# Issuing the rotary half copies from SyncE, and a planned order that runs the transposes of one PSUM tile in a row

## The chip, the cores and the metric

The kernel runs on one core of a Trainium2 chip. The core has five instruction queues that run side by side: TensorE (PE in the profile, with its weight loads shown apart as PEld), VectorE (DVE), ScalarE (ACT), GpSimd (POOL) and SyncE (SP), which here only issues DMAs. Each queue works through its instructions in the order in which they stand in the program; between queues, semaphores hold an instruction until its inputs are there. [...]

The metric is the device time of one execution in microseconds, as the median of three runs.

## What is computed

A two-layer backbone over 512 latent tokens and 256 context tokens of width 1024. Each layer normalises its input, projects it once into the queries, keys and values of three groups of heads and a gate, runs the three kinds of attention, multiplies by the gate and projects back:

```
def layer(x, cx, c_silu, cctx_silu, norm_w, ada_w, ada_b, w_in, w_out, qn, kn, rpb, sink, cos, sin, need_ctx):
    ...
    hx = rmsnorm(x, norm_w) * (1 + scale[:, None, :]) + shift[:, None, :]
    hc = rmsnorm(cx, norm_w) * (1 + scale_c) + shift_c
    px = split_cols(hx @ w_in)
    pc = split_cols(hc @ w_in)
    ya, yca = global_gqa(px[0], px[1], px[2], pc[0], pc[1], pc[2], cos, sin, qn, kn, need_ctx)
    yb, ycb = neighbourhood_attn(px[3], px[4], px[5], pc[3], pc[4], pc[5], rpb, need_ctx)
    yc_, ycc = window_gqa(px[6], px[7], px[8], pc[6], pc[7], pc[8], cos, sin, sink, need_ctx)
    ux = jnp.concatenate([ya, yb, yc_], axis=-1) * jax.nn.silu(px[9])
    x = x + gate[:, None, :] * (ux @ w_out)
```

Group A is global attention, group B attends to a two-dimensional neighbourhood, group C to a sliding window; all three also attend to the context. The queries and keys of A and C are rotated by position:

```
def apply_rope(x, cos, sin):
    x1, x2 = jnp.split(x, 2, axis=-1)
    ...
    return jnp.concatenate([x1 * c - x2 * s, x1 * s + x2 * c], axis=-1)
```

The first layer also updates the context; the second only reads it.

## The kernel before

**Numbers.** A float32 operand is kept as two parts (a rounded part and the rest), and a product takes three matmuls, rounded by rounded, rounded by rest and rest by rounded. The rounded part is made by ACT, the rest mostly by DVE or POOL.

**Stages.** The weights arrive in tiles of 256 KB (`ws`, line 251, and `ws` of the output projection, line 497), issued by SP into three buffers; ACT makes the rounded part `wh` (line 242), and DVE or POOL the rest `wl` (line 245), which frees the buffer. Projections run into two PSUM banks called `pj` (lines 308 and 329). The attention of one head runs in units: scores into `Sbig` (line 1028), a maximum on DVE (`negm`, lines 1133, 1183 and 1240), Exp on ACT into a tile `P` (lines 1135, 1186 and 1242), transposes of 128 x 128 blocks of `P` on PE into a PSUM tile `T` (line 1031, two banks), a copy out of `T` into a rounded part `pth` on ACT (line 778) and a rest `ptl` on DVE (line 1024), and the product with the values into `Obig` (line 1028). ACT's `otmp` (line 1046) and a sum on DVE take that product out. At the end of a pair of heads the gate and the sums of Exp are applied, again by way of transposes into `T` (lines 1326 and 1333 read them). Projections of later pairs are woven between these units, so that PE has work while it waits for an attention step.

**A tile of transposes.** In global attention a `T` tile takes four transposes, two from each of the two `P` tiles of a unit; in the other two groups two to four, from as many `P` tiles. These are float32 against `ident`. Queries and keys of group A are turned as well, in the rounded type against `identr` (lines 840 and 879), four to a tile. All four of a tile stand together in the program as written.

**Rotation of group C.** For a tile of queries or keys, ACT copies the projection out of PSUM into `tA` (line 953). A rotation needs the other half of each head, which lies in other partitions, so four DMAs of 32 partitions and 64 KB each copy `tA` into `tB` with the halves exchanged (line 958). POOL then multiplies `tA` and `tB` by the tables of cosines and sines and adds (lines 959 to 961); ACT and POOL make the two parts of the query from that (lines 969 and 970) or of the key (lines 979 to 981). There are ten such tiles: in each layer one of keys and four of queries. `tA` and `tB` have one buffer each, which the rotation of group A uses too.

**The order.** What each queue does first is not the order of the program text. After the whole program is recorded, `arrange` makes a `Step` of every instruction, with a cost (`Step.cost`: how long it holds its engine, `busy`, and when its result is there, `last`; for a DMA `busy` is the issue), builds the graph of what must come before what (`Graph.__init__`), and plays the program through (`Graph.run`): at each moment an engine takes the ready step of the best rank. Ranks come from playing the graph backwards from the end (`Graph.back`). This is done six times, and the order of the play with the earliest end is fixed as the order of every queue, the DMA issues of SP and ACT included.

Of the kernel before, what the change touches and what calls it, by code (L numbers as in the profile page):

```python
# [751 lines left out]
def mixers(tc, nc, l, last, p1, ps, const, env):  # L752
# [192 lines left out]
    def rope_c(s, scale, need_ctx, bank):  # L945
        q = p1.tile([128, NT], F32, name="tA", bufs=CFG["tA"])
        r = slot("tR")

        def done(p, c0, n):
            if c0:  # L950
                nc.scalar.activation(r[:, NT:NA], p, AF.Copy, scale=scale)
            else:
                nc.scalar.activation(rowmajor(q), colmajor(p), AF.Copy, scale=scale)  # L953

        yield from proj_f(l, s, need_ctx, bank, done)
        sw = p1.tile([128, NT], F32, name="tB", bufs=CFG["tA"])
        for b in range(4):
            nc.scalar.dma_start(sw[b * 32:(b + 1) * 32], q[(b ^ 1) * 32:((b ^ 1) + 1) * 32])  # L958
        en("cr0").tensor_mul(r[:, 0:NT], q, tabs["C", 0])
        en("cr1").tensor_mul(sw, sw, tabs["C", 1])  # L960
        en("cr2").tensor_add(r[:, 0:NT], r[:, 0:NT], sw)
        return r
# [511 lines left out]
    prev = None  # L1474
# [24 lines left out]
    for pair, items, n_ada in PLAN:  # L1499
# [3 lines left out]
        if pair is not None:  # L1503
            kind, i = pair
            if kind == "B":
                Q, K = made["b", i]
                prev = units("B", i, Q, K, made["v", i // 2][i % 2], lambda i=i: made["g", i // 2][i % 2], bmb)
            else:
                Q, G = made[kind.lower(), i]
                K, V = made[kind.lower() + "kv", 0]  # L1510
                prev = units(kind, i, Q, K, V, G, bmc if kind == "C" else None)
# [13 lines left out]
    prev = units("C", 3, Q, K, V, G, bmc)  # L1525
# [22 lines left out]
POOLS = ("p0_", "p1_0_", "p2_0_", "p1_1_", "p2_1_")  # L1548
BANKS = ("pj", "T", "Sbig", "Obig")
TO_PE, TO_OTHER, FIXED, RATE = 400.0, 150.0, 2550.0, 395.0  # L1550
WAIT = {"PE": 53.0, "POOL": 78.0, "ACT": 36.0, "DVE": 36.0, "SP": 30.0}
BEHIND = {"ACT": 112.0, "DVE": 85.0, "POOL": 45.0}


def stem(name):
    return name.rsplit("_", 1)[0]
# [9 lines left out]
class Step:  # L1566
# [16 lines left out]
    def cost(self):  # L1583
        ins = [u for u in self.use if not u[1]]
        outs = [u for u in self.use if u[1]]
        n = max([size(u[2]) for u in ins + outs[:1]] or [0])
        bank = any(stem(u[0].name) in BANKS for u in ins)
        op = str(getattr(self.inst, "op", getattr(self.inst, "func", ""))).split(".")[-1]
        e = self.engine
        self.plain = False  # L1590
        if self.dma:
            b = 4 * outs[0][2][0][1] * size(outs[0][2])
            self.busy = 330.0 if e == "SP" else 260.0
            self.move = 3460.0 if stem(outs[0][0].name) == "bc" else b / RATE
        elif e == "PE":
            n = size(ins[0][2])
            self.exact = ins[0][4] == "float32"
            self.busy = (108.0 if n == 128 else 230.0) if self.exact else max(n / 2.4 + 13.5, 66.0)
            self.last = 272.0 if self.exact else n / 2.4 + 180.0
        else:  # L1600
            if e == "ACT":
                d = 172.0 + 0.83 * n + (0 if bank else 35)
            elif e == "DVE":
                d = 156.0 + 0.52 * n if self.kind == "InstTensorCopy" and not bank else 152.0 + 1.06 * n
                self.plain = self.kind == "InstTensorTensor" and not bank and n >= 256
            elif op == "pow":
                d = 1000.0
            elif self.kind == "InstTensorScalarPtr":
                d = 440.0 + 2.2 * n if n > 8 else 190.0
            else:  # L1610
                d = 190.0 + 2.14 * n if n > 64 else 150.0
            self.busy = max(d - BEHIND[e], 20.0)
            self.last = d
            if e == "ACT" and op == "Exp" and n > 12:
                self.busy, self.last = d - 16, d + 91
# [18 lines left out]
class Graph:  # L1634


    def __init__(self, steps, tiles, needed):
        self.steps = steps
        n = len(steps)
        at = {s.name: k for k, s in enumerate(steps)}  # L1640
        self.before = [{} for _ in steps]
        seen, known, users, first = {}, {}, {}, {}
        for k, s in enumerate(steps):
            for tensor, writes, ap, offset, _ in s.use:
                name = tensor.name
                u = users.setdefault(name, [])
                if not u or u[-1] != k:
                    u.append(k)
                if name not in tiles or tiles[name][1]:
                    region, strict = None, writes  # L1650
                elif stem(name) in BANKS:
                    region, strict = (0, 128, 1), 1
                else:
                    if (ap, offset) not in known:
                        known[ap, offset] = cells(ap, offset)
                    region, strict = known[ap, offset], writes
                keep = []
                for rec in seen.get(name, ()):
                    r, st, w, j = rec
                    hit = region is None or (r[0] < region[1] and region[0] < r[1] and r[2] & region[2])  # L1660
                    if hit and (st or strict) and j != k:
                        t = steps[j]
                        full = 1
                        if t.engine == s.engine and not (t.dma or s.dma):
                            full = int(s.engine != "PE" and w)
                        elif region is None and w and writes:
                            full = 0
                        self.before[k][j] = max(full, self.before[k].get(j, 0))
                    over = (region is not None and hit and strict and region[0] <= r[0] and r[1] <= region[1]
                            and r[2] | region[2] == region[2])  # L1670
                    if not over or j == k:
                        keep.append(rec)
                keep.append((region, strict, writes, k))
                seen[name] = keep
        for a, b in needed:
            self.before[at[a]].setdefault(at[b], 0)
        self.users = {name: u for name, u in users.items() if name in tiles and not tiles[name][1]}
        for u in self.users.values():
            for k in u[1:]:
                self.before[k].setdefault(u[0], 0)  # L1680
        self.after = [[] for _ in steps]
        for k, b in enumerate(self.before):
            for j in b:
                self.after[j].append(k)
        self.tag = {name: tiles[name][0] for name in self.users}
        self.order = {}
        for name, u in sorted(self.users.items(), key=lambda x: x[1][0]):
            self.order.setdefault(self.tag[name], []).append(name)
        self.room = {t: min(CAPS.get(t.split("_")[0], 1), len(v)) for t, v in self.order.items()}
        self.place = {name: i for v in self.order.values() for i, name in enumerate(v)}  # L1690
        self.pool = {t: next((i for i, p in enumerate(POOLS) if "_" + p in t + "_"), None) for t in self.order}
        self.opens = [[] for _ in steps]
        for name, u in self.users.items():
            self.opens[u[0]].append(name)
        self.touch = [{u[0].name for u in s.use if u[0].name in self.users} for s in steps]

    def run(self, rank):

        steps, n = self.steps, len(self.steps)
# [4 lines left out]
        now = {e: [] for e in ENGINES.values()}  # L1704
# [8 lines left out]
            if self.pool[t] is not None:  # L1713
                stage_left[self.pool[t]] += len(v)
        lanes, pipe = [], 0.0
        done = 0

        def push(k):
            heapq.heappush(later[steps[k].engine], (ready[k], rank[k], k))
# [9 lines left out]
        while done < n:  # L1729
            t, e = min((max(free[e], -1.0 if now[e] else later[e][0][0]), e) for e in later if now[e] or later[e])  # L1730
            free[e] = t = max(t, free[e])
            while later[e] and later[e][0][0] <= t:
                _, r, k = heapq.heappop(later[e])
                heapq.heappush(now[e], (r, k))
            r, k = heapq.heappop(now[e])
            s = steps[k]
            need, wait = t, None
# [24 lines left out]
            busy = s.busy  # L1762
            if s.dma:
                pipe = fin = max(t + FIXED, pipe) + s.move
                lanes.append(fin)
            elif e == "PE":
                fin = t + s.last
            else:
                extra = 0.55 * min(free["POOL"] - t, s.last) if s.plain and free["POOL"] > t else 0.0
                fin = t + s.last + extra  # L1770
                busy += extra
# [18 lines left out]
            for j in self.after[k]:  # L1790
                x = fin + self.gap(s, steps[j]) if self.before[j][k] else t
# [173 lines left out]
```

## Time and profile before

| | |
|---|---|
| median of three runs | 1178.56 us (1177.38 to 1178.78) |
| profiled execution | 1178.53 us |
| its span, first to last instruction | 1176.3 us |
| mean granted TensorE clock | 0.996 |
| matmuls | 8016 |
| transposes in float32 of `P` (line 1031) | 1024 |
| transposes of group A's queries and keys (lines 840, 879) | 48 and 80 |
| copies of rotary halves | 40, on ACT's queue |

In rows of busy time an engine's figure is the time in which at least one of its instructions runs, with the count behind an x. Matmuls overlap: one of 256 columns is drawn 0.28 us long and the next may start 0.12 us after it. In a timeline row stand the start, the length, the engine (with a q where its sequencer issues or waits and the engine itself does nothing), the line, the operation, the tiles as out<-in, the shapes and the count; in square brackets is the idle time of that engine just before, and what ended it. In a row of waits stand who waited, for whom, the sum in us, how often, and the longest.

### The profile page before, as it was taken

What the parts mean: (1) busy time and instruction counts of PE and PEld (TensorE: products, weight loads), DVE (VectorE), ACT (ScalarE), POOL (GpSimd) and SP (SyncE); (2) the same over time, 40 slices, a digit from 0 to 9 for tenths busy, and PEclk for the clock granted to TensorE, in tenths of its full rate; (3) what the DMA queues carried; (4) which work ended last, traced back from release to release, by engine and by line L of the source; (5) the groups of instructions that cost most, each with busy time, mean ns of one, the idle gap of its engine ahead of it and who ended that gap; (6) DMA issues with size and microseconds to landing.
All of it is one profiled execution on the core that took longest, in us unless ns stands there. A gap on an engine that the chain in (4) does not pass through costs nothing. (4 is left out here: it accounts for less than half of the span.)

```text
span 1176.3 us, 21720 instructions
## 1 busy us (share of the span) xinstructions
PE 1141.1 (97%) x8016; PEld 1028.0 (87%) x8016; DVE 766.3 (65%) x1548; ACT 697.8 (59%) x1581; POOL 401.7 (34%) x496
## 2 busy tenths in 40 slices
PE   5999999999999999999999999999999999999996
PEld 3799989998898898988788999989988989898885
DVE  5667666665455665657979855676665566668652
ACT  5447555566557666678723634555656677778641
POOL 2442111125445456367300030221235665466001
PEclk9999999999999999999999999999999999999998
DMA  9633222213222222122577432233221121123152
GB/s 359 209 99 99 83 70 95 101 55 112 81 69 96 72 77 86 59 64 91 157 253 265 153 129 88 88 98 98 88 79 60 58 72 53 57 63 108 37 170 72
DMA packets 60825, 124.21 MB, mean 106 GB/s; under 512 B 7216, under 2 KB 13488, under 8 KB 60720
## 3 DMA queue, kind: packets, MB, share of 16 engines
q1 hardware_dynamic: 54768, 111.96, 29.8%
q10 hardware_dynamic: 5952, 10.88, 2.8%
q8 instruction: 63, 1.03, 0.4%
q14 instruction: 42, 0.34, 0.1%
HBM read 109.05 MB, written 11.14 MB: 102 GB/s over the span
## 5 line engine op out<-in xcount | busy, mean ns | idle before, releaser
L1024 DVE TENSOR_TENSOR ptl<-T,pth 128x512 fp32r<-128x512 f32 (+2 forms) x312 | 181.4, 591 | 119.3 <-ACT pth L778 114.7
L778 ACT ACTIVATE pth<-T 128x512 fp32r<-128x512 f32 (+2 forms) x312 | 160.7, 522 | 103.5 <-PE T L1031 93.1
L329 PE MATMUL pj<-wh,hL 128*128 128x256 f32 x896 | 189.2, 289 | 0.2 <-DVE vt L854 0.2
L308 PE MATMUL pj<-hL,wh 128*128 128x512 f32 x544 | 186.4, 405 | 0.0
L1031 PE MATMUL T<-ident,P 128*128 128x128 f32 x1024 | 177.9, 274 | 5.7 <-DVE ptl L1024 2.8
L1028 PE MATMUL Sbig<-kt,qt 128*128 128x256 f32 (+1 forms) x864 | 162.0, 309 | 1.2 <-DVE negm L1240 0.8
L242 ACT ACTIVATE wh<-ws 128x512 fp32r<-128x512 f32 x192 | 120.2, 630 | 67.3 <-PE pj L308 16.2
L1031 PEld LDWEIGHTS T<-ident,P 128*128 128x128 f32 x1024 | 124.8, 140 | 29.3 <-DVE ptl L1024 8.1
L329 PEld LDWEIGHTS pj<-wh,hL 128*128 128x128 f32 x896 | 147.3, 190 | 2.1 <-issue 1.3
L245 POOL TENSOR_TENSOR wl<-ws,wh 128x512 fp32r<-128x512 f32 x76 | 98.4, 1300 | 122.4 <-ACT wh L242 115.6
L1028 PE MATMUL Obig<-ptl,vt 128*128 128x256 f32 (+2 forms) x432 | 131.1, 317 | 1.4 <-DVE ptl L1024 1.4
L1028 PEld LDWEIGHTS Sbig<-kt,qt 128*128 128x128 f32 x864 | 124.8, 189 | 7.8 <-DVE negm L1240 1.4
L1028 PE MATMUL Obig<-pth,vt 128*128 128x256 f32 (+2 forms) x432 | 130.0, 309 | 1.4 <-ACT pth L778 1.2
L329 PE MATMUL pj<-wl,hL 128*128 128x256 f32 x448 | 128.3, 287 | 0.0
L245 DVE TENSOR_TENSOR wl<-ws,wh 128x512 fp32r<-128x512 f32 x116 | 82.5, 721 | 41.7 <-ACT wh L242 31.9
L308 PEld LDWEIGHTS pj<-hL,wh 128*128 128x128 f32 x544 | 97.1, 189 | 13.9 <-ACT wh L242 0.4
L308 PE MATMUL pj<-hL,wl 128*128 128x512 f32 x272 | 109.0, 401 | 0.1
L1028 PEld LDWEIGHTS Obig<-pth,vt 128*128 128x128 f32 x432 | 81.8, 189 | 7.8 <-ACT pth L778 2.0
L1028 PEld LDWEIGHTS Obig<-ptl,vt 128*128 128x128 f32 x432 | 81.6, 189 | 6.6 <-DVE ptl L1024 2.2
L329 PEld LDWEIGHTS pj<-wl,hL 128*128 128x128 f32 x448 | 85.2, 190 | 1.0 <-issue 0.4
L1413 POOL TENSOR_TENSOR bm<-wr,bm 128x192 f32<-128x192 f32 (+1 forms) x48 | 36.6, 789 | 136.5 <-DMA bm<-mskB_dram 73.2
L1047 DVE TENSOR_TENSOR OT<-Obig,otmp 64x512 f32<-64x512 f32 (+1 forms) x88 | 45.1, 512 | 49.2 <-ACT otmp L1046 48.3
(336 smaller groups left out, 2522.5 us busy)
## 6 DMA issues: line engine op xcount, KB each, us to landing
ws<-wf_dram SPq DMA_DIRECT2D x72, 256.0 KB, 2.9
ws<-wt_dram SPq DMA_DIRECT2D x72, 256.0 KB, 2.9
ada<-adaw_dram SPq DMA_DIRECT2D x32, 512.0 KB, 5.5
ws<-wo_dram SPq DMA_DIRECT2D x57, 256.0 KB, 2.9
bm<-mskB_dram SPq DMA_DIRECT2D x16, 576.0 KB, 3.5
dots<-adat_dram SPq DMA_DIRECT2D x16, 256.0 KB, 3.1
dw<-adat_dram SPq DMA_DIRECT2D x8, 512.0 KB, 7.3
u<-u ACTq DMA_DIRECT2D x9, 384.0 KB, 2.5
```

What stands on the lines that cost most here:

```text
L242: nc.scalar.activation(hi, src, AF.Copy)
L245: eng.tensor_sub(lo, src, hi.bitcast(F32))
L308: nc.tensor.matmul(p[:, 0:n], a[:, r, :], cols(b[kt], c0, n), start=(i == 0), stop=(i == 23))
L329: nc.tensor.matmul(p[:, t * 256:(t + 1) * 256], tok(a[kt], t2 + t), b[:, r, :], start=(i == 0), stop=(i == 23))
L778: nc.scalar.activation(out, src, AF.Copy)
L1024: nc.vector.tensor_sub(lo[:, 0:n], T[:, 0:n], hi[:, 0:n].bitcast(F32))
L1028: return nc.tensor.matmul(*args, **kw)
L1031: return nc.tensor.transpose(*args, **kw)
L1047: nc.vector.tensor_add(OT[64 * h:64 * h + 64, c0:c0 + n], O[0:64, 0:n], tmp[:, 0:n])
L1413: nc.gpsimd.tensor_add(b, src, b)
```

## The change

Line 958 issues the four copies from `nc.sync` in place of `nc.scalar`. All else is in the planner:

- The cost of a DMA issue was 330 ns on SP and 260 ns on ACT. It is now looked up by the name of the tile written: 580 for `tB`, 680 for `wr`, 430 for all other tiles here (no tile of this kernel is named `R5` or `R2`).
- A matmul of 128 columns in the rounded type holds PE for 65.3 ns in the plan, where it was 66.8. Where a matmul follows a transpose, 5 ns (float32) or 86 ns (rounded type) are added.
- Transposes that stand together in the program and write the same PSUM tile form a run. Each of them now has to wait for all that any of them needs, and while one of a run has just been taken, the plan takes the next ready one of the same run before anything else.

```diff
--- before.py
+++ after.py
@@ -955,7 +955,7 @@
         yield from proj_f(l, s, need_ctx, bank, done)
         sw = p1.tile([128, NT], F32, name="tB", bufs=CFG["tA"])
         for b in range(4):
-            nc.scalar.dma_start(sw[b * 32:(b + 1) * 32], q[(b ^ 1) * 32:((b ^ 1) + 1) * 32])
+            nc.sync.dma_start(sw[b * 32:(b + 1) * 32], q[(b ^ 1) * 32:((b ^ 1) + 1) * 32])
         en("cr0").tensor_mul(r[:, 0:NT], q, tabs["C", 0])
         en("cr1").tensor_mul(sw, sw, tabs["C", 1])
         en("cr2").tensor_add(r[:, 0:NT], r[:, 0:NT], sw)
@@ -1548,6 +1548,7 @@
 POOLS = ("p0_", "p1_0_", "p2_0_", "p1_1_", "p2_1_")
 BANKS = ("pj", "T", "Sbig", "Obig")
 TO_PE, TO_OTHER, FIXED, RATE = 400.0, 150.0, 2550.0, 395.0
+ISSUE = dict(tB=580.0, R5=520.0, R2=520.0, wr=680.0)
 WAIT = {"PE": 53.0, "POOL": 78.0, "ACT": 36.0, "DVE": 36.0, "SP": 30.0}
 BEHIND = {"ACT": 112.0, "DVE": 85.0, "POOL": 45.0}
 
@@ -1587,16 +1588,18 @@
         bank = any(stem(u[0].name) in BANKS for u in ins)
         op = str(getattr(self.inst, "op", getattr(self.inst, "func", ""))).split(".")[-1]
         e = self.engine
-        self.plain = False
+        self.plain, self.turn, self.switch = False, None, 0.0
         if self.dma:
             b = 4 * outs[0][2][0][1] * size(outs[0][2])
-            self.busy = 330.0 if e == "SP" else 260.0
+            self.busy = ISSUE.get(stem(outs[0][0].name).split("_")[0], 430.0)
             self.move = 3460.0 if stem(outs[0][0].name) == "bc" else b / RATE
         elif e == "PE":
             n = size(ins[0][2])
-            self.exact = ins[0][4] == "float32"
-            self.busy = (108.0 if n == 128 else 230.0) if self.exact else max(n / 2.4 + 13.5, 66.0)
-            self.last = 272.0 if self.exact else n / 2.4 + 180.0
+            exact = ins[0][4] == "float32"
+            self.turn = outs[0][0].name if stem(ins[0][0].name) in ("ident", "identr") and n == 128 else None
+            self.switch = 5.0 if exact else 86.0
+            self.busy = (108.0 if n == 128 else 230.0) if exact else n / 2.4 + (13.5 if n > 128 else 12.0)
+            self.last = 272.0 if exact else n / 2.4 + 180.0
         else:
             if e == "ACT":
                 d = 172.0 + 0.83 * n + (0 if bank else 35)
@@ -1674,6 +1677,20 @@
                 seen[name] = keep
         for a, b in needed:
             self.before[at[a]].setdefault(at[b], 0)
+        run = []
+        for k in [k for k, s in enumerate(steps) if s.engine == "PE"] + [None]:
+            if run and (k is None or steps[k].turn is None or steps[k].turn != steps[run[0]].turn):
+                whole = {}
+                for i in run:
+                    for j, full in self.before[i].items():
+                        if j < run[0]:
+                            whole[j] = max(full, whole.get(j, 0))
+                for i in run:
+                    for j, full in whole.items():
+                        self.before[i][j] = max(full, self.before[i].get(j, 0))
+                run = []
+            if k is not None and steps[k].turn:
+                run.append(k)
         self.users = {name: u for name, u in users.items() if name in tiles and not tiles[name][1]}
         for u in self.users.values():
             for k in u[1:]:
@@ -1713,7 +1730,7 @@
             if self.pool[t] is not None:
                 stage_left[self.pool[t]] += len(v)
         lanes, pipe = [], 0.0
-        done = 0
+        prev, done = None, 0
 
         def push(k):
             heapq.heappush(later[steps[k].engine], (ready[k], rank[k], k))
@@ -1732,6 +1749,12 @@
             while later[e] and later[e][0][0] <= t:
                 _, r, k = heapq.heappop(later[e])
                 heapq.heappush(now[e], (r, k))
+            if e == "PE" and prev is not None and prev.turn:
+                same = [x for x in now[e] if steps[x[1]].turn == prev.turn]
+                if same:
+                    now[e].remove(min(same))
+                    heapq.heapify(now[e])
+                    heapq.heappush(now[e], ((-1e18, 0), min(same)[1]))
             r, k = heapq.heappop(now[e])
             s = steps[k]
             need, wait = t, None
@@ -1765,6 +1788,10 @@
                 lanes.append(fin)
             elif e == "PE":
                 fin = t + s.last
+                if not s.turn and prev is not None and prev.turn:
+                    busy += prev.switch
+                    fin += prev.switch
+                prev = s
             else:
                 extra = 0.55 * min(free["POOL"] - t, s.last) if s.plain and free["POOL"] > t else 0.0
                 fin = t + s.last + extra
```

## The prediction

> **What bounds the kernel now.** I read the page's first two parts, then the busy time by stretch, the list of DMA issues, the line of the half copies, and the timeline around each of their bursts.
>
> ```profile
> PE 1141.1 (97%) x8016; PEld 1028.0 (87%) x8016; DVE 766.3 (65%) x1548; ACT 697.8 (59%) x1581; POOL 401.7 (34%) x496
> ```
>
> ```profile
> 0.00:30.00 30.00, 17.10 (x108) 9.90 (x108) 17.80 (x52) 16.27 (x36) 7.19 (x12) 1.00 0.97 359
> 30.00:1160.00 1130.00, 1118.46 (x7869) 1013.24 (x7868) 744.22 (x1487) 680.38 (x1543) 389.68 (x478) 1.00 0.31 99
> 1160.00:1176.30 16.30, 5.58 (x43) 4.86 (x41) 4.26 (x9) 1.19 (x3) 4.84 (x7) 0.68 0.38 129
> ```
>
> PE is busy for 97% of the span, at a granted clock of 1.00 (the third number from the right) until the last stretch. The change leaves every matmul in place, so it can win only where PE waits. The rows by stretch say where: 30.00 - 17.10 = 12.90 us at the start, where the DMA engines are 97% busy; 16.30 - 5.58 = 10.72 us in the closing chain; and 1130.00 - 1118.46 = 11.54 us in the whole middle. Start and end have no rotary copy and hardly a transpose. So what this change can win lies in those 11.54 us, plus a little that the rows hide: a 256-column matmul is drawn 0.28 us long while the next one starts 0.12 us after it, so every idle figure is about 0.16 us short of what PE loses.
>
> **Part one: the half copies leave ACT.**
>
> ```profile
> L958 ACTq DMA_DIRECT2D tB<-tA x40: 514/593/858, 275.8 to 1065.2; - x40
> ...
> DMA to landing us min/median/max: 1.9/2.0/3.8
> ```
>
> Ten rotary tiles with four copies each are 40 issues with a median of 593 ns; a tile's four hold ACT for about 2.4 us, 24 us in all. ACT has room for that over the span (59% busy), but it does its work in a fixed order, and what stands behind a burst is late by the burst. This is the worst one:
>
> ```profile
> 878.39 2.46 ACTq L958 DMA_DIRECT2D tB<-tA  x4
> ...
> 879.90 0.28 PE L308 MATMUL pj<-hC,wh 128*128 128x256 f32 x1
> 880.90 0.38 ACT L778 ACTIVATE pth<-T 128x256 fp32r<-128x256 f32 x1 [2.54 <-DMA tB<-tA]
> ...
> 881.33 0.39 PE L1028 MATMUL Obig<-pth,vt 128*128 128x256 f32 x1 [1.16 <-ACT pth L778]
> ```
>
> ACT issues from 878.39 to 880.85; only then can it copy a transposed tile out of PSUM (pth), and PE, which needs pth, has nothing from 879.90 + 0.12 until 881.33: 1.31 us lost, where the row shows 1.16 idle. Four other bursts end in a wait of PE:
>
> ```profile
> 278.38 0.38 ACT L1046 ACTIVATE otmp<-Obig 64x256 f32<-64x256 f32 x1 [1.85 <-DMA tB<-tA]
> ...
> 279.81 0.63 PE L1031 MATMUL T<-ident,P 128*128 128x128 f32 x4 [0.88 <-DVE u L1333]
> ```
>
> ```profile
> 376.53 0.38 ACT L1046 ACTIVATE otmp<-Obig 64x256 f32<-64x256 f32 x1 [2.54 <-DMA tB<-tA]
> ...
> 377.96 0.63 PE L1031 MATMUL T<-ident,P 128*128 128x128 f32 x4 [0.94 <-DVE OT L1326]
> ```
>
> ```profile
> 526.57 0.60 ACT L778 ACTIVATE pth<-T 128x512 fp32r<-128x512 f32 x1 [1.25 <-issue]
> ...
> 527.95 0.66 PE L1031 MATMUL T<-ident,P 128*128 128x128 f32 x4 [0.64 <-DVE ptl L1024]
> ```
>
> ```profile
> 955.50 0.50 PE L1028 MATMUL Sbig<-kt,qt 128*128 128x256 f32 x2 [0.42 <-ACT P L1135]
> ```
>
> In the first two ACT's otmp stands behind the burst, DVE's sum behind otmp, and a PSUM bank that DVE must read first behind that; in the third ptl stands behind a pth that ACT took up between two issues; in the fourth the Exp of line 1135 came late. Idle: 1.16 + 0.88 + 0.94 + 0.64 + 0.42 = 4.04 us, and with 5 x 0.16 us hidden, 4.8 us. The other five bursts show no wait of PE that carries a sum; I round to **5 us**. All of it should go, since in these rows nothing but the issues keeps ACT. What is late next at those places I cannot see; if it is late by half as much, 2.5 us remain of the gain. Those are the ends for this part: 2.5 and 5.5.
>
> **What SP pays.** SP issues its own loads at 0.33 us each and otherwise waits:
>
> ```profile
> 872.62 0.33 SPq L251 DMA_DIRECT2D ws<-wf_dram  x1
> 883.20 17.65 SPq L251 DMA_DIRECT2D ws<-wt_dram  x4
> ```
>
> ```profile
> SPq L251 <- POOL wl L245: 298.5, 52, 21.9
> ```
>
> Around the worst burst SP has nothing to issue from 872.95 to 883.20. No row shows such a copy on SP; I take ACT's 0.59 us, so 24 us on a queue that spent 298.5 us on one kind of wait alone. Behind a copy that waits for its tile (line 953, on ACT) stand the weight loads, and for them ACT's split; a burst delays them by 2.4 us, and those loads are queued several tiles ahead. I cost it at nothing; without that cover it would be 2.4 us for a tile. The other way round, a copy may stand behind a load that waits up to 21.9 us for its buffer. Who waits for a late copy is POOL's rotation, then the query tile, then PE's band scores:
>
> ```profile
> 909.45 2.45 ACTq L958 DMA_DIRECT2D tB<-tA  x4
> ...
> 918.66 1.29 POOL L970 TENSOR_TENSOR qt<-tR,qt 64x512 fp32r<-64x512 f32 x1
> ...
> 920.42 0.28 PE L1028 MATMUL Sbig<-kt,qt 128*128 128x256 f32 x1
> ```
>
> ```profile
> 1082.26 1.29 POOL L970 TENSOR_TENSOR qt<-tR,qt 64x512 fp32r<-64x512 f32 x1 [0.52 <-ACT qt L969]
> ...
> 1091.36 0.88 DVE L1183 CUSTOM_DVE_ANT_0 P<-Sbig,msk,negsink 128x640 f32<-128x640 f32 x1
> ```
>
> The first query tile of layer 1 is ready at 919.95, and PE reads it 0.47 us later; the last one is ready at 1083.55, and the first reduction of its scores starts 7.8 us later. So the copies have cover everywhere but at 909, and there the price of landing at the slow end (3.8 against 2.0 us) is 1.8 - 0.47 = 1.3 us at most, if PE finds nothing else; it has projection matmuls, so I take 0.
>
> A rule speaks against the move. The Trainium skill, "DMA: Bandwidth & Descriptors", section "Issuing engines are not separate DMA queues", says that DMAs share the same 16 DMA engines whoever issues them, and that spreading them saves only issue time; its section on queues, rings and completion order adds that an engine alternates between queue rows and starts one row's descriptors in order. The landing row (2.0 median, 3.8 at most) fits the sharing. By the rule a copy on SP's row starts behind a weight load instead of beside it, and the sum would lose up to that same 1.3 us at 909 and nothing elsewhere.
>
> **Part two: the order.** The planner's costs change for every DMA issue, and the transposes of one PSUM tile now run in a row, none before all their inputs are there. First what a broken row costs PE:
>
> ```profile
> 916.56 0.60 PE L1031 MATMUL T<-ident,P 128*128 128x128 f32 x4
> ...
> 917.48 0.27 PE L1031 MATMUL T<-ident,P 128*128 128x128 f32 x1
> 917.50 0.36 PE L329 MATMUL pj<-wh,hL 128*128 128x256 f32 x1
> 917.71 0.28 PE L329 MATMUL pj<-wl,hL 128*128 128x256 f32 x1
> ```
>
> ```profile
> 236.11 0.22 PE L840 MATMUL T<-identr,qd 128*128 128x128 f32 x1
> 236.17 0.34 PE L329 MATMUL pj<-wl,hC 128*128 128x256 f32 x1
> 236.34 0.28 PE L329 MATMUL pj<-wh,hC 128*128 128x256 f32 x1
> ...
> 236.81 0.37 PE L840 MATMUL T<-identr,qd 128*128 128x128 f32 x3
> ```
>
> Within a row a float32 transpose takes (0.60 - 0.27)/3 = 0.11 us. A single one between matmuls takes 917.71 - 917.48 - 0.12 = 0.11 us as well: breaking a row costs nothing. With identr it is (0.37 - 0.22)/2 = 0.075 us in a row and 236.34 - 236.11 - 0.12 = 0.11 us alone, 0.035 us for a break; there are 128 of them in 32 tiles, and if every one stood alone the 96 breaks would be worth 3.4 us. Most stand in threes and fours in the stretches I read; I take **0.5 us**, between 0 and 3.4.
>
> Against that stands a wait. A global-attention tile takes its transposes from two probability tiles, and the second is ready one Exp later:
>
> ```profile
> L1135 ACT ACTIVATE P<-Sbig,negm 128x768 f32<-128x768 f32 x64 | 57.7, 901 | 22.4 <-DVE negm L1133 20.5 <-ACT wh L242 0.8 <-DVE ptl L1024 0.6
> L1135 ACT ACTIVATION_READ_ACCUMULATOR P<-Sbig,negm 128x1 f32 x64 | 12.6, 197 | 0.0
> ```
>
> That is 0.90 + 0.20 = 1.10 us in each of 64/2 = 32 pairs: 35 us if PE had nothing else, 0 if projection matmuls fill it. Now they fill nearly everything (11.54 us idle in 1130), and the planner places its rows with that filler, so I take 0 and keep a quarter of the pairs, 8 x 1.1 = 8.8 us, as the far end that I would still believe. Behind a waiting transpose all of PE's later work stands; next it is pth and ptl.
>
> Last, the new costs re-sort all queues. What an order leaves outside the five waits is 11.54 - 4.04 = 7.5 us; a new order draws this anew, between 0 and twice that. I take no change.
>
> Sum against the profiled execution's own 1178.53 us (span 1176.3 and 2.2 around it; the median of the runs, 1178.56, is the same): 1178.53 - 5.0 - 0.5 = 1173.0 us.
>
> **The rivals.**
> - **The new order also fills other waits.** Most of the 7.5 us goes, because the planner's picture of the queues is truer: 1173.0 - 5 = 1168.0 us. For it: the waits at the bursts look like errors of its picture. Against it: what is left is small waits on DVE, which the change does not cost anew.
> - **The order gives the gain back.** ACT, freed, meets DVE or a PSUM bank a little later, and about as much new idle time appears elsewhere: 1173.0 + 4.5 = 1177.5 us. For it: with two T banks and one Obig the chain has little play. Against it: PE ran through the other five bursts with hardly a wait.
> - **The rows hold PE (slower).** Place: the first transposes of a pair's tile in global attention, where PE has to wait for the second Exp. Price 1.10 us for each pair without filler; the 5.5 us are gone from the fifth, and the time is over 1180.9 from the eighth: 1173.0 + 8.8 = 1181.8 us. Against it: the filler is there in both layers.
> - **A copy is late on SP's queue** at 909, by the queue or by a load in front: 1173.0 + 1.3 = 1174.3 us; a load that holds it by 10 us would cost more, but the planner orders SP by the same times.
>
> **How the numbers follow.** Forecast 0.45 (1170.5 to 1175.8), fills other waits 0.17 (around 1168), late copy 0.06 (1174.3), gain given back 0.18 (1177.5), rows hold PE 0.14 (1181.8). About 0.2%, 2.4 us, is what a measurement can tell from no change, so faster is below 1176.2 and slower above 1180.9. Faster: 0.45 + 0.17 + 0.06 = 0.68, to which the given-back case adds 0.02 from its low end: 0.70. Same: the rest of that case, 0.16. Slower: 0.14. The range runs from 1166.5 (the second case less 1.5) to 1181.8 (eight pairs held), leaving about 0.07 below and 0.11 above.
>
> **What would show it.** In the profile after: the line of the copies on SPq, 40 of them; no ACT row whose idle time ends with a copy's issue; PE's idle time in the middle at about 6 to 7 us; the transposes of a tile in one row of four or three. Wrong would be: PE waits on P of line 1135 in front of rows of transposes (the slower case), as much idle time in the middle as before with other releasers (given back), POOL's line 960 waiting long for the copies with PE idle at the first band scores (late copy), or a start or end stretch that moves, which I costed at nothing.

## The result, and the profile after

The median of five runs is 1174.18 us (1172.83 to 1175.16) against 1178.56 us before: a ratio of 0.9962, with a 95% interval from 0.9950 to 0.9974. The forecast was 1173.0 us. The time was foreseen, but the profile after does not look as the forecast said. The page's busy time, and the busy time by stretch (columns as before):

```profile
PE 1138.2 (97%) x8016; PEld 1031.2 (88%) x8016; DVE 764.4 (65%) x1548; ACT 699.5 (60%) x1581; POOL 405.6 (35%) x496
```

```profile
0.00:30.00 30.00, 16.31 (x114) 9.36 (x116) 18.05 (x53) 17.03 (x37) 9.03 (x12) 1.00 0.96 351
30.00:1156.00 1126.00, 1115.53 (x7861) 1016.29 (x7856) 742.02 (x1487) 681.20 (x1542) 391.74 (x478) 1.00 0.31 99
1156.00:1172.40 16.40, 6.32 (x48) 5.59 (x47) 4.33 (x9) 1.30 (x4) 4.86 (x7) 0.75 0.37 128
```

The span fell by 3.9 us, from 1176.3 to 1172.4. In the middle stretch PE is idle for 1126.00 - 1115.53 = 10.47 us, where it was 11.54 and where I had expected 6 to 7. Start and end changed by 0.8 us up and 0.6 us down. The other 3.0 us are in PE's busy time, which also holds waits too short to show beside the drawn length of a matmul. At the five bursts of the forecast PE no longer waits, but other waits came. The largest of the new ones, in the timeline of after:

```profile
277.10 2.49 SPq L958 DMA_DIRECT2D tB<-tA  x4
...
279.69 0.72 SPq L195 DMA_DIRECT2D ada<-adaw_dram  x1
...
280.67 0.33 SPq L251 DMA_DIRECT2D ws<-wt_dram  x1
...
283.63 1.27 POOL L960 TENSOR_TENSOR tB<-tB,tabx 128x512 f32<-128x512 f32 x1 [2.99 <-DMA tB<-tA]
...
288.68 1.71 ACT L979 ACTIVATE kt<-tR 64x768 fp32r<-64x768 f32 x2 [3.08 <-POOL tR L961]
...
289.61 4.49 POOL L980 TENSOR_TENSOR kt<-tR,kt 64x768 fp32r<-64x768 f32 x2 [0.96 <-ACT kt L979]
...
291.47 0.95 DVE L981 CAST kt<-kt 64x1536 fp32r<-64x1536 f32 x1 [5.15 <-POOL kt L980]
292.46 0.42 DVE L1047 TENSOR_TENSOR OT<-Obig,otmp 64x256 f32<-64x256 f32 x1
...
292.93 0.38 PE L1028 MATMUL Obig<-pth,vt 128*128 128x256 f32 x1 [1.61 <-DVE OT L1047]
...
293.76 0.55 PE L308 MATMUL pj<-hC,wh 128*128 128x256 f32 x1 [0.45 <-DVE mod L221]
```

This is layer 0's tile of rotary keys. Its copies are issued on SP by 279.59, but POOL gets the last of them only at 283.6, 4 us later, with a 512 KB load and a weight load in flight beside it. From there the delay walks down the chain: POOL's rotation, ACT's rounded key, POOL's rest, and DVE's copy of line 981. DVE works in order and stood idle for 5.15 us in front of that copy, with the sum of line 1047 behind it; PE could not write `Obig` until that sum had read it, and its next projection waited 0.45 us more for DVE's line 221. Then the clock fell (columns: the stretch and its length, PE's busy time and count, granted clock, DMA share, GB/s):

```profile
290.00:292.00 2.00, 1.32 (x11) 1.00 0.00 0
292.00:294.00 2.00, 0.62 (x2) 0.92 0.00 0
294.00:296.00 2.00, 2.00 (x10) 0.50 0.00 0
296.00:298.00 2.00, 2.00 (x15) 0.73 0.00 0
298.00:300.00 2.00, 2.00 (x19) 1.00 0.03 8
```

From 294 to 296 PE is drawn busy all the time and gets 10 matmuls done, against 19 in the 2 us from 298, at full clock. A stretch like this counts as busy, so PE's idle time alone hides it.

### The profile page after: what moved, and what is told of

Its sections match the earlier page's. It is cut to its first block, busy times and chain, and to the rows that moved or that the text cites. A ratio compares the mean times of both kernels' runs of the same rounds, so it can differ in the third digit from the quotient of the medians.

```text
span 1172.4 us, 21741 instructions
## 1 busy us (share of the span) xinstructions
PE 1138.2 (97%) x8016; PEld 1031.2 (88%) x8016; DVE 764.4 (65%) x1548; ACT 699.5 (60%) x1581; POOL 405.6 (35%) x496
## 5 line engine op out<-in xcount | busy, mean ns | idle before, releaser
L329 PE MATMUL pj<-wh,hL 128*128 128x256 f32 x896 | 186.0, 286 | 0.0
L308 PE MATMUL pj<-hL,wh 128*128 128x512 f32 x544 | 181.4, 401 | 0.0
L1031 PE MATMUL T<-ident,P 128*128 128x128 f32 x1024 | 162.4, 274 | 5.4 <-DVE ptl L1024 4.3
L1031 PEld LDWEIGHTS T<-ident,P 128*128 128x128 f32 x1024 | 121.4, 140 | 26.2 <-DVE ptl L1024 8.4
L1133 DVE TENSOR_REDUCE negm<-Sbig 128x1 f32<-128x768 f32 x64 | 61.1, 955 | 28.2 <-ACT P L1135 14.8
```

The source lines that it names most:

```text
L308: nc.tensor.matmul(p[:, 0:n], a[:, r, :], cols(b[kt], c0, n), start=(i == 0), stop=(i == 23))
L329: nc.tensor.matmul(p[:, t * 256:(t + 1) * 256], tok(a[kt], t2 + t), b[:, r, :], start=(i == 0), stop=(i == 23))
L1031: return nc.tensor.transpose(*args, **kw)
L1133: nc.vector.tensor_reduce(nm, S, axis=AX.X, op=OP.max, negate=True)
```

## The experiments

The theory was that of the forecast: ACT's issues held PE. Its rivals were the rows of transposes, the late copy, and the costs by which the order is made. All times are medians against runs of the kernel before on the same chip, whose medians were 1178.98, 1179.07 and 1179.64 us in the three groups; ratios are used to compare across groups.

| run | time us | ratio to before | 95% interval |
|---|---|---|---|
| e1 order of before, 40 copies on SP | 1178.87 | 0.9994 | 0.9983 to 1.0004 |
| e2 order of after, 40 copies on ACT | 1173.01 | 0.9950 | 0.9937 to 0.9962 |
| e4 after without the rule for rows | 1171.44 | 0.9938 | 0.9925 to 0.9950 |
| e5 rule for rows alone | 1184.39 | 1.0048 | 1.0034 to 1.0061 |
| e7 order of after, layer 0's key tile on ACT | 1171.37 | 0.9937 | 0.9924 to 0.9949 |
| e8 order of before, 36 copies on SP | 1173.16 | 0.9953 | 0.9941 to 0.9966 |
| e9 issue costs alone | 1168.32 | 0.9913 | 0.9899 to 0.9926 |
| e10 costs of PE alone | 1180.66 | 1.0015 | 1.0007 to 1.0024 |
| e11 issue costs and the move | 1173.33 | 0.9943 | 0.9930 to 0.9955 |
| e12 cost of a copy alone | 1170.07 | 0.9919 | 0.9906 to 0.9933 |
| e13 issue costs with 330 for the rest | 1171.35 | 0.9926 | 0.9913 to 0.9938 |
| e14 order of e9, 36 copies on SP | 1169.10 | 0.9909 | 0.9896 to 0.9923 |

**e1: the move and nothing else.** The plan is made as before, with the copies on ACT; then they are taken out of ACT's queue and put into SP's by their planned start. Every other queue keeps its order, so nothing but the move differs.

```diff
+        self.half = self.dma and any(u[1] and stem(u[0].name) == "tB" for u in self.use)
+        if self.half:
+            self.engine = "ACT"
...
-    for ks in best[1].values():
+    streams, start = best[1], best[2]
+    halves = [k for k in streams["ACT"] if steps[k].half]
+    streams["ACT"] = [k for k in streams["ACT"] if not steps[k].half]
+    streams["SP"] = sorted(streams["SP"] + halves, key=lambda k: (start[k], k))
+    for ks in streams.values():
```

> Every queue keeps the order of before; only the 40 copies leave ACT's queue and stand in SP's at the place that their planned start gives. Theory (the issues on ACT held PE): 1178.6 - 4.8, so 1173 to 1174.5 us, and PE's idle time in the middle stretch falls from 11.5 to about 7 us. Rival (the gain came from the new order, above all from fewer broken rows of transposes): 1177.5 to 1179 us.

Measured: no change, 0.9994. Taken alone that would fell the theory, but the waits show two things at once. PE's waits from 850 to 1060 us, first of before, then of e1:

```profile
PE Obig L1028 <- ACT pth L778: 1.2, 1, 1.2
PE Obig L1028 <- DVE ptl L1024: 1.0, 2, 0.5
PE Sbig L1028 <- ACT P L1135: 0.4, 1, 0.4
PE pj L329 <- DVE vt L854: 0.2, 1, 0.2
```

```profile
PE Obig L1028 <- DVE ptl L1024: 1.4, 2, 0.9
PE pj L329 <- DVE vt L854: 0.2, 1, 0.2
```

The waits on ACT are gone. But at layer 0's key tile there is this, in the timeline of e1:

```profile
275.93 1.85 SPq L958 DMA_DIRECT2D tB<-tA  x3
...
277.83 0.58 SPq L195 DMA_DIRECT2D ada<-adaw_dram  x1
278.45 0.51 SPq L958 DMA_DIRECT2D tB<-tA  x1
...
284.75 1.29 POOL L960 TENSOR_TENSOR tB<-tB,tabx 128x512 f32<-128x512 f32 x1 [4.46 <-DMA tB<-tA]
...
291.55 0.38 ACT L1046 ACTIVATE otmp<-Obig 64x256 f32<-64x256 f32 x1
...
291.96 0.42 DVE L1047 TENSOR_TENSOR OT<-Obig,otmp 64x256 f32<-64x256 f32 x1 [5.62 <-ACT otmp L1046]
...
294.55 0.47 PE L308 MATMUL pj<-hC,wh 128*128 128x256 f32 x2 [2.83 <-DVE mod L221]
```

and in the stretches after it (columns as above):

```profile
294.00:298.00 4.00, 3.45 (x19) 0.65 0.00 0
...
575.00:578.00 3.00, 3.00 (x12) 0.52 0.31 97
```

The copies' landing times in e1 (minimum, median, maximum):

```profile
DMA to landing us min/median/max: 1.9/2.0/6.1
```

Three copies go out, a 512 KB load slips in between, and POOL gets the fourth only at 284.75, 6 us after its issue. The chain differs a little from that of after: ACT's rounded key runs until 291.52 and holds ACT's otmp, DVE stands idle for 5.62 us in front of its sum, and lines 981, 1024 and 221 follow in DVE's order. It ends in 2.83 us of idle PE and a stretch at half clock. A second fall of the clock comes at 575, behind this wait:

```profile
573.70 0.88 PE L1031 MATMUL T<-ident,P 128*128 128x128 f32 x6 [1.95 <-DVE ptl L1024]
```

The kernel before has the same wait with 1.74 us, at 572.91, and keeps its clock there; nothing shows that the second fall has to do with the late copy.

**e2: the reverse,** with the order of after and the copies put back on ACT in the same way.

> Every queue keeps the order of after; only the 40 copies are put back into ACT's queue at their planned start. Theory (the issues on ACT held PE): 1174.2 + 4 to 6, so 1178 to 1180 us. Rival (new order): 1173.5 to 1176 us, and less if the copies land sooner on ACT's own queue.

Measured: 1173.01 us, no slower than after (0.9950 against 0.9962, and the intervals overlap). So what after gained over before does not come from the move, taken as a whole. This is the rival's case.

**e4 and e5: the rule for rows,** taken out of after, and put alone into before. The edit is the block of `run` in `Graph.__init__` and the choice in `Graph.run`:

```diff
-            if e == "PE" and prev is not None and prev.turn:
-                same = [x for x in now[e] if steps[x[1]].turn == prev.turn]
...
```

> The changed kernel without the rule that keeps the transposes of a tile in a row; copies on SP, new costs, planned anew. Theory (the copies): 1173 to 1175.5 us, as the rule costs and gains next to nothing. Rival (rows): 1177 to 1179 us.

> The kernel of before with the rule for rows alone: copies on ACT, old costs, planned anew. Theory (the copies): 1177 to 1180 us. Rival (rows): 1173.5 to 1175.5 us.

Measured: without the rule the changed kernel is faster (1171.44, below both expectations), and the rule alone makes the kernel of before slower (1184.39). Both theories had expected otherwise of e5. The middle of e5 (PE's busy time alone), and the waits of PE that the slower rival of the forecast would have made:

```profile
30.00:1166.00 1136.00, 1120.24 (x7866) 1.00 0.31 98
```

```profile
PE T L1031 <- ACT P L1135: 1.1, 2, 0.8
```

PE idles 15.76 us there, 4.2 more than before. Only 1.1 us are waits of transposes for an Exp of line 1135, and 0.8 us of these stand behind a burst of copies on ACT, which held that Exp.

```profile
310.17 2.44 ACTq L958 DMA_DIRECT2D tB<-tA  x4
...
312.66 0.90 ACT L1135 ACTIVATE P<-Sbig,negm 128x768 f32<-128x768 f32 x1 [2.52 <-issue]
...
313.70 0.55 PE L1031 MATMUL T<-ident,P 128*128 128x128 f32 x3 [0.80 <-ACT P L1135]
```

Six waits of PE in e5 follow such a burst (at 282.33, 313.70, 379.71, 456.90, 535.58 and 961.25), together 5.60 us, where the five of before came to 4.04. So some 1.6 of the 4.2 us come from copies that the new order placed worse; the others are spread over many lines and releasers. With the rule the kernel is slower, but how much of that is the rule's own waiting was not settled.

For after the rival is the key tile. The list of PE's waits of after has no transpose that waits for line 1135. In e4 the copies landed within 3.5 us, where the slowest of after took 4.8, and PE lost less behind the key:

```profile
293.91 0.50 PE L308 MATMUL pj<-hC,wh 128*128 128x256 f32 x2 [0.93 <-ACT tR L988]
```

That is 0.93 us and no fall of the clock there, against 1.61 + 0.45 us and a fall in after. This can be the whole difference between e4 and after.

**e7 and e8: the late copy.** The orders of after and of before again, with one difference: the four copies of layer 0's key tile go out from ACT, the other 36 from SP.

```diff
-            nc.sync.dma_start(sw[b * 32:(b + 1) * 32], q[(b ^ 1) * 32:((b ^ 1) + 1) * 32])
+            (nc.scalar if l == 0 and s == WF_CK else nc.sync).dma_start(sw[b * 32:(b + 1) * 32], q[(b ^ 1) * 32:((b ^ 1) + 1) * 32])
```

> The order of after on every queue; only the four copies of layer 0's key tile go back to ACT's queue. Theory (late copy: on SP's queue the fourth copy of that tile lands 4.5 us after its issue, POOL, ACT and DVE run late behind it, PE idles 1.6 + 0.5 us at 291 to 294 and then runs 3.4 us at half the granted clock): that stall and the half clock go, 1174.2 less 2.5 to 4 us, so 1170 to 1172 us. Rival (the key tile has nothing to do with it, or the stall moves on): 1173.5 to 1175 us.

> The order of before on every queue; 36 copies on SP, the four of layer 0's key tile stay on ACT. Theory (late copy: in the run with all 40 on SP the fourth copy of that tile stands behind a 512 KB load and lands 6.1 us after its issue, PE idles 2.8 us at 291.7 and runs 3.4 us at half clock): the gain of the move shows, 1174 to 1176 us, and no wait of PE on mod of line 221. Rival (taking the issues off ACT is worth nothing): 1178 to 1179.5 us.

Measured: 1171.37 us, as expected, and 1173.16, a little below it. Four issues of forty make the difference between nothing and 0.9953 in the old order, and between 0.9962 and 0.9937 in the new one. The 36 copies alone bring little in the order of after (e7 at 0.9937 against e2 at 0.9950, within the noise), and e7 still has the rule for rows but is as fast as e4. In e8 PE's idle time in the middle is 8.19 us, and its clock stays whole:

```profile
30.00:1154.00 1124.00, 1115.81 (x7870) 1.00 0.31 99
```

```profile
290.00:300.00 10.00, 9.79 (x73) 1.00 0.09 28
570.00:580.00 10.00, 9.37 (x58) 1.00 0.40 136
```

**e9 and e10: the two kinds of new costs, each alone.** Copies on ACT, no rule for rows; e9 has the line with `ISSUE`, e10 the costs of PE.

> The kernel of before with the new issue costs alone (580 for the copies, 680 for wr, 430 else), copies on ACT, planned anew. Theory (the true issue costs make the better order): 1171.5 to 1175 us. Rival 1 (the costs of PE do): 1177.5 to 1180 us. Rival 2 (any re-sorting draws a new order, good or bad by chance): anywhere from 1170 to 1185 us, and then the parts do not add up.

> The kernel of before with the new costs of PE alone (5 or 86 ns after a transpose, 65.3 ns for 128 columns), no rule for rows, copies on ACT, planned anew. Theory (true issue costs): 1177.5 to 1180 us. Rival 1 (PE costs): 1171.5 to 1175 us. Rival 2 (chance): anywhere from 1170 to 1185 us.

Measured: 1168.32 us for e9, lower than even the theory expected and by the ratios some 5.8 us below the changed kernel, though every copy is still issued by ACT; 1180.66 us for e10, a little above the theory's range. PE's idle time in the middle of e9 is 1120.00 - 1113.38 = 6.62 us:

```profile
30.00:1150.00 1120.00, 1113.38 (x7864) 1.00 0.31 100
```

How the plan did it is seen at the burst that was the worst of before, in the timeline of e9 (ACT's rows alone):

```profile
873.66 1.18 ACTq L958 DMA_DIRECT2D tB<-tA  x2
874.89 0.39 ACT L778 ACTIVATE pth<-T 128x256 fp32r<-128x256 f32 x1 [0.83 <-PE T L1031]
874.91 0.57 ACTq L958 DMA_DIRECT2D tB<-tA  x1
875.58 0.39 ACT L778 ACTIVATE pth<-T 128x256 fp32r<-128x256 f32 x1 [0.31 <-PE T L1031]
875.86 0.90 ACT L1135 ACTIVATE P<-Sbig,negm 128x768 f32<-128x768 f32 x1
876.49 0.51 ACTq L958 DMA_DIRECT2D tB<-tA  x1
```

The four issues no longer stand in one block. Two go out, then a pth, one issue, a pth and an Exp, and the last issue; at both pth ACT was waiting for PE, not the other way round. The rows also show that an instruction of ACT that has begun runs on beside an issue: the first pth lasts from 874.89 to 875.28, and the issue next to it begins at 874.91. It is the instruction behind the issue that waits.

PE's idle time is not all of what e9 won. Its span is 10.3 us shorter than that of before, and 5.4 us of this lie in PE's busy time (1141.14 against 1135.78 us); what makes them up was not settled.

**e11: the move on top of the issue costs.**

> The new issue costs and the move to SP, planned anew, without the new costs of PE and without the rule for rows. Theory (once the plan knows what an issue costs, ACT can carry the copies, and SP's queue adds late landings): 1169 to 1173 us, slower than the issue costs alone (1168.3). Rival 1 (the move is worth its 5 us on top): 1163 to 1166 us. Rival 2 (a new order is a draw): anywhere from 1165 to 1180 us.

Measured: 1173.33 us, slower than e9 and a little above the theory's 1173. The late key tile is back:

```profile
294.00 0.38 PE L1028 MATMUL Obig<-pth,vt 128*128 128x256 f32 x1 [1.90 <-DVE OT L1047]
...
294.69 0.30 PE L1031 MATMUL T<-ident,P 128*128 128x128 f32 x1 [0.31 <-DVE mod L221]
```

That is 2.2 us where e9 has 0.4 in the same stretch; the clock stayed whole. **e12 to e14** ask what in the issue costs does it, and what is left for the move.

```diff
-            self.busy = 330.0 if e == "SP" else 260.0
+            self.busy = 580.0 if stem(outs[0][0].name) == "tB" else 330.0 if e == "SP" else 260.0
```

> The kernel of before with one number changed: the plan costs each half copy on ACT at 580 ns in place of 260; all other issues as before; planned anew. Theory (the plan's error of 4 x 0.32 us a burst made the waits): most of what the issue costs alone gave, 1168 to 1172 us. Rival (the other issues' costs did it): 1176 to 1179.5 us. Rival 2 (a draw): anywhere from 1165 to 1180 us.

> The issue costs alone with 330 in place of 430 for all issues but the copies and wr, nearer to the 0.33 us of the trace; copies on ACT. Theory (a truer plan is a better order): 1167 to 1170 us. Rival (a draw): anywhere from 1165 to 1180 us, and then what a single re-sorting gives or takes is several us without any cause in its costs.

> The order of the run with the issue costs alone on every queue; 36 copies put on SP at their planned start, layer 0's key tile stays on ACT. Theory: its plan already keeps the copies out of the way, so little is left to win: 1167.5 to 1170 us. Rival (each issue on ACT costs PE time): 1163 to 1166 us.

Measured: 1170.07, 1171.35 and 1169.10 us. One number, 580 for 260, gives 0.9919, nearly all of what e9 has. With 330 for all other issues, which is nearer to the trace, it is 0.9926: a little outside what was expected, and not better than with 430. Taking 36 copies off ACT in the order of e9 gives nothing more (0.9909 against 0.9913). e9 and e14 have the lowest medians of this study, and both are faster than before and after.

The ratios make a ladder from before to after: the issue costs 0.9913 (e9), with the move 0.9943 (e11), with the costs of PE 0.9938 (e4), with the rule for rows 0.9962 (after). In microseconds of 1178.56 that is -10.3, +3.5, -0.6 and +2.8, together -4.5 before rounding. Each ratio is uncertain by some 1.5 us and a step between two of them by about 2 us. So the -10.3 is clear, the +3.5 and the +2.8 lie outside their noise but not far, and the -0.6 cannot be told from nothing. Every step is also a new order, in which layer 0's key tile may come out otherwise.

## Why the prediction came out right, and which of its steps failed

- **PE bounds the kernel, and only its waits can be won: held.** The idle time of the middle goes with the time by and large: 6.62 us in e9, 11.54 before, 15.76 in e5. But the idle time of the rows is not all: stretches at half clock count as busy, and half of what e9 won lies in PE's busy time.
- **Five microseconds for the bursts on ACT: the mechanism held, where it is let act.** e8 shows 0.9953, 5.5 us (4.0 to 7.0), with the order of before kept on the other queues, and its list of PE's waits from 300 to 1060 us names neither ACT's pth nor line 1326 any more. But it moves four of the five bursts. The key tile's burst stays on ACT with its wait of 0.88 us (at 280.19), and the other four were priced at 3.16 + 4 x 0.16 = 3.8 us. So the size was, if anything, priced too low.
- **"So the copies have cover everywhere but at 909": this step failed.** I had looked at query tiles only and followed them to PE. Layer 0's key tile has no such cover: behind its copies stand not only the key but ACT's otmp (e1) and DVE's line 981 (after), and behind those, in DVE's fixed order, a sum and a reduction that PE waits for. I priced a late copy at 1.3 us at most. By after and e7 it is 2.9 us; by e1 and e8 it is (0.9994 - 0.9953) x 1178.6 = 4.8 us, but there the second fall of the clock, at 575, is in the difference. The rule of the Trainium skill that spoke against the move ("DMA: Bandwidth & Descriptors", "Issuing engines are not separate DMA queues") says that DMAs of all issuers run on the same 16 DMA engines, and that another issuer saves issue time alone. The landings agree: 2.0 us at the median from ACT's queue (before) and from SP's (after). The fourth copy of e1, issued behind the 512 KB load, came 4 us later than that. It was my cover that was wrong, and with it the 1.3 us.
- **The rows of transposes: 0 taken, 0.5 us gained for identr. Not borne out, and its cost is open.** With the rule alone the kernel of before is 0.48%, 5.7 us slower, inside the far end of 8.8 us that I had kept. The place that I gave it, the second Exp of a pair, accounts for 1.1 us, of which 0.8 stand behind a burst of copies. In after the step is 2.8 us (0.9962 against 0.9938), and the key tile alone can explain that. No run shows the 0.5 us.
- **"The new costs re-sort all queues ... I take no change": this step failed most.** The largest term of the sum was missing. The issue costs alone are worth 10.3 us. The waits at the bursts were errors of the plan, as my first rival said: a plan that knows of the 580 ns can lay the issues between ACT's other work. That accounts for PE's lost idle time, 4.9 of the 10.3 us; the cause of the other 5.4 stays open. I had counted that as a rival beside the move (1168.0 us, 0.17). It is in fact the same gain won in another way, and more: e12 shows 0.9919 from the 580 alone.
- **The sum: 5.5 us forecast, 4.4 measured, and made of other terms.** That the total came out near is luck: what the order won by the issue costs was given back in part by the late key tile, and perhaps by the rows.

How much of a single order is chance is only bounded: e9, e12 and e13 differ in the costs of issues that hardly matter, and lie within 0.0013 of each other, 1.5 us. The 0.6 us of PE's costs in the ladder is below that. Alone (e10) they cost 1.8 us, but the profiled execution of e10 also runs 6.8 us of its start at half clock, so these need not come from the order.

## What to carry to other kernels

Where an instruction is in the way because a plan costs it too low, give the plan the measured cost first; moving it to another queue may then win nothing (e14), and with layer 0's key tile among the moved copies it lost 3.5 us here (e11). Before moving a DMA to a queue that carries large loads, follow every reader of what it brings, and in each reader's queue the instructions that stand behind it, up to the engine that bounds the kernel. A right total is no proof of its terms: keep the order of all other queues fixed in one experiment, so that the moved part is seen alone.

## What the runs showed of the hardware that was not expected

The granted clock of TensorE halved after some short waits. In after it fell when PE had been idle 1.61 and 0.45 us with one matmul between, in e1 after 2.83 us and again after 1.95. It stayed at 0.50 for about 3.4 us: in after the three stretches from 292 to 298 lack (0.08 + 0.50 + 0.27) x 2 us = 1.7 us of full clock, and at 0.50 that takes 1.7 / 0.50 us. In that time matmuls of 256 columns started 0.21 us apart in place of 0.12:

```profile
295.61 0.41 PE L1028 MATMUL Obig<-ptl,vt 128*128 128x256 f32 x1
295.82 0.41 PE L1028 MATMUL Obig<-pth,vt 128*128 128x256 f32 x1
296.04 0.41 PE L1028 MATMUL Obig<-ptl,vt 128*128 128x256 f32 x1
```

The Trainium skill ("TensorE: Matmul & The Clock Gate", part 1 on the clock gate) tells of a fall to half rate after an idle window of about 3.4 us. Here less than that of idle time was enough, while the kernel before had a wait of 1.74 us on ptl in its middle without any fall, and e11 had 1.90 and 0.31 us, more in sum than after, without one. So I estimate that a wait of about 2 us may cost PE some 1.7 us more behind it (half of 3.4 us), and whether it does is not seen from its length alone.
